# Pooling product of a hybrid decoder layer: fp32 operands, or operands split into two parts with three passes

## The chip, the cores and the metric

The kernel runs on one core of one Trainium2 chip. The metric is the device time of one execution in microseconds (us). A core has a matrix engine (PE, TensorE) with its weight loads (PEld), a vector engine (DVE), a scalar engine (ACT), a further engine (POOL) and one that mostly issues transfers (SP). The engines work side by side and wait for one another through semaphores.

## The reference

One decoder layer over 1024 positions of width 1024: a token-mixing sub-layer, a squared-ReLU MLP, and a last norm. The token mixing has a part that the change touches, a pooling mixer over 256 channels, and beside it a gated recurrence over 768 channels.

```python
def pool_mixer(u, w, scale):
    # u: (B, S, 256); w: (4, 64, 64); scale: (256,)
    for gi, win in enumerate((2, 4, 8, 16)):
        lo, hi = gi * 64, (gi + 1) * 64
        win_sum = c[:, :, lo:hi] - cp[:, MAX_WIN - win:MAX_WIN - win + S, lo:hi]
        cnt = jnp.minimum(t + 1, win)
        groups.append(win_sum / cnt - uf[:, :, lo:hi])
    p = jnp.stack(groups, axis=2)
    y = jnp.einsum('bsgc,gcd->bsgd', p, w).reshape(B, S, 256)
    return y * scale

h = rms_norm(x, norm_mix_g); u = h @ w_in
x = x + concat([pool_mixer(...), hgrn2_mixer(...)]) @ w_out
h2 = rms_norm(x, norm_mlp_g)
x = x + square(relu(h2 @ w_up)) @ w_down
return rms_norm(x, final_norm_g)
```

Here `c` is the running sum of the pooling inputs over positions: each output is the mean over a trailing window less the token itself, multiplied by a 64 x 64 matrix of its group. All inputs and the output are float32.

## The kernel before

The kernel works on tiles of 128 partitions. Its large products don't multiply fp32 operands directly. `split` (lines 116 to 119) makes two parts of an operand, a rounded high part with an ACT cast to fp32r and a low part with a DVE subtract, and `mm3` (lines 121 to 126) multiplies high by high, high by low and low by high into one PSUM bank: three matmuls, seen in the profile as lines 124, 125 and 126.

The work has three large stages. The first projects the normed input with `w_in` and runs the recurrence head by head (0 to 372 us of the span), with the output projection `w_out` at its end and after it. The second is the product with `w_up`, the third that with `w_down`.

In the first stage the six heads run one after another. Each head's recurrence (`hgrn`, line 394) is cut into the steps near, middle, far, keys, updates and output. Dense products that later heads need (`beside`, line 602) are dealt out between the steps by a table of lags, so TensorE has dense matmuls while DVE and ACT prepare the next step. The order on TensorE is written out by hand in all of this. The order on DVE and ACT is written out only in the opening part (lines 643 to 723), which ends with the first preparations of head 0; after it a planner places their instructions by its own estimate of when each is ready, and may also put prefetches between those of the opening part.

The pooling part has two tiles of 128 channels, `kt` 0 and 1. `pool_input` (line 555) loads its columns of `w_in` as a split weight, runs the dense product for both halves of the positions (shown as `ps_pool`), and builds the windows on DVE by doubling (lines 561 to 574), ending with a multiply-subtract at line 571. `pool_output` (line 577) multiplies the windows by `pw`, a block-diagonal 128 x 128 matrix that holds two groups, 512 positions at a time (line 581), and ACT scales the result into `mix` (line 584). Tile 0 is prepared beside head 4, and multiplied beside head 5, after the gate of head 4. Tile 1 is prepared next, and multiplied after 12 of the 16 steps of the gate of head 5. `pw` is zeroed at line 241 and loaded with four small transfers on SP at line 721.

The parts of weights live in a ring of four turns for each part (pool `wsplit`, line 152, tags `whi` and `wlo`, filled by `load_w`, line 156). From there the blocks of `w_out` come too: four blocks at lines 747 and 748, in the order that `MIX_ORDER` (line 37) needs them. The scores' PSUM banks (`score_ps`, two of them) are used by the pooling product as well.

After the last gate, `mix` is split into `mT` (line 752), and TensorE begins the output rows (`ps_o`), 2, 3 and 4 of the mixing blocks first, then the transposes of the last head, then blocks 5, 6, 0, 1 and 7.

Of the kernel before, what the change touches and what calls it, by code (L numbers as in the profile page):

```python
# [11 lines left out]
F32R = mybir.dt.float32r  # L12
# [5 lines left out]
P = 128  # L18
S = 1024
# [43 lines left out]
def kernel(  # L63
# [20 lines left out]
    pe, act, dve, pool = nc.tensor, nc.scalar, nc.vector, nc.gpsimd  # L84
# [31 lines left out]
    def split(hi, lo, src):  # L116

        act.copy(hi, src)  # L118
        dve.tensor_tensor(out=lo, in0=src, in1=hi.bitcast(F32), op=ALU.subtract)  # L119

    def mm3(ps, lhs, rhs, start, stop, goes_on=False):

        (lh, ll), (rh, rl) = lhs, rhs
        pe.matmul(ps, lh, rh, start=start, stop=False, skip_group_check=goes_on)  # L124
        pe.matmul(ps, lh, rl, start=False, stop=False, skip_group_check=goes_on)  # L125
        pe.matmul(ps, ll, rh, start=False, stop=stop, skip_group_check=goes_on)  # L126
# [24 lines left out]
    wring = {"raw": [], "split": [], "n": 0}  # L151
# [28 lines left out]
    with ExitStack() as pa:  # L180
        cmix = pa.enter_context(tc.tile_pool(name="cmix", bufs=1))
# [8 lines left out]
        lb = cmix.tile([P, NH], F32, name="lb")  # L190
        om = cmix.tile([P, NH], F32, name="om")
        pw = cmix.tile([P, 2, P], F32, name="pw")
        ha = pa.enter_context(tc.tile_pool(name="ha", bufs=2))
        HALF = S // 2
        V0 = POOL_W + 2 * HW
# [148 lines left out]
        def col_tile(c0, name, raw=None, parts=split):  # L344
            return load_w(w_in_v[:, :, c0:c0 + P], [KT, P], name, raw=raw, parts=parts)

        def dense_T(dst, w, h, name):

            ps = dense_ps(f"ps_{name}_{h}")
            for j in range(KT):  # L350
                mm3(ps, (w[0][:, j, :], w[1][:, j, :]), (hT[h][0][:, j, :], hT[h][1][:, j, :]), j == 0, j == KT - 1)
                yield
            rv, pv = rms_row[:, h * HALF:(h + 1) * HALF], ps
            if len(dst.shape) == 3:
                rv, pv = rv.rearrange("p (c t) -> p c t", t=P), pv.rearrange("p (c t) -> p c t", t=P)
            dve.tensor_tensor(out=dst, in0=pv, in1=rv, op=ALU.mult)
            return ps
# [197 lines left out]
        def pool_input(kt, wins):  # L555
            u = ha.tile([P, S], F32, tag="GQ"[kt], name=f"u_{kt}", bufs=1 + kt)
            w = col_tile(kt * P, f"pool{kt}")
            for h in range(2):
                yield from dense_T(by_chunk(u, h), w, h, f"pool{kt}")
            prev = u  # L560
            for lev in range(2 * kt + 2):
                sh = 1 << lev
                w = wins[lev % 2]
                dve.tensor_copy(w[:, :sh], prev[:, :sh])
                dve.tensor_tensor(out=w[:, sh:], in0=prev[:, sh:], in1=prev[:, :S - sh], op=ALU.add)
                prev = w
            for e in range(2):
                pr = slice(e * 64, (e + 1) * 64)
                w = wins[e]
                dve.tensor_tensor(out=w[pr, :PAD], in0=w[pr, :PAD], in1=pconst[pr, kt, :PAD], op=ALU.mult)  # L570
                dve.scalar_tensor_tensor(
                    out=wins[0][pr, :], in0=w[pr, :], scalar=pconst[pr, kt, PAD:], in1=u[pr, :],
                    op0=ALU.mult, op1=ALU.subtract,
                )
            return wins[0]

        def pool_output(kt, u):
            t = ha.tile([P, S], F32, tag="V", name=f"mix_{kt}", bufs=3)
            for b in range(2):
                ps = score_ps(f"psp_{kt}_{b}")  # L580
                pe.matmul(ps, pw[:, kt, :], u[:, b * 512:(b + 1) * 512], start=True, stop=True)
                for h in range(2):
                    c0 = h * 512 + b * 256
                    act.mul(
                        t[:, c0:c0 + 256].rearrange("p (c t) -> p c t", t=P), by_chunk(ps, h), pscale[:, kt:kt + 1]
                    )
            mix[kt] = t
# [55 lines left out]
        with tc.manual_schedule(engines={mybir.EngineType.PE, mybir.EngineType.DVE, mybir.EngineType.Activation}):  # L643
            for j in load_xt(0, (("Q", 2), ("Q", 2), ("K", 2), ("K", 2))):
                xt_hi(0, j)
                if j % 4 == 0:
                    raw = wraw.tile([P, 4, 256], F32, tag="raw", name=f"raw_v0_{j // 4}")
                    w0.append([wring["split"][0].tile([P, 4, 256], F32R, tag=f"w{part}", name=f"w{part}_v0_{j // 4}") for part in ("hi", "lo")])

                n = 1 if j < 2 else 2 if j % 2 == 0 else 0  # L650
                if n:
                    ks = slice(j % 4, j % 4 + n)
                    nc.sync.dma_start(raw[:, ks], w_in_v[:, j:j + n, V0:V0 + 256])
                    split(w0[-1][0][:, ks], w0[-1][1][:, ks], raw[:, ks])
                xt_lo(0, j)
            wq = q_weights(0, early_raw("T", "q_0"), put_off)
            xns = [load_rows(i) for i in range(2)]
            wf = f_weights(0, early_raw("Kn", "f0"), put_off)
            xns += [load_rows(i) for i in range(2, 4)]
            for _ in load_xt(1, (("F", 1), ("V", 3), ("G", 1), ("S", 1))):  # L660
                pass
            xns += [load_rows(i) for i in range(4, NT)]
            split(*later.pop(0))


            mx = small.tile([P, NH], F32, tag="lbt", name="lb_shift")
            dve.tensor_tensor(out=mx, in0=lbl, in1=lbl, op=ALU.subtract)
            ex = small.tile([P, NH], F32, tag="lbt", name="lb_exp")
            act.activation(ex, mx, AF.Exp)
            rc = small.tile([P, NH], F32, tag="lbt", name="lb_rcp")  # L670
            dve.reciprocal(rc, ex)
            sm = small.tile([P, NH], F32, tag="lbt", name="lb_soft")
            dve.tensor_tensor(out=sm, in0=ex, in1=rc, op=ALU.mult)
            dve.tensor_tensor(out=lb, in0=sm, in1=sm, op=ALU.subtract)
            dve.tensor_scalar(om, lb, -1.0, 1.0, op0=ALU.mult, op1=ALU.add)

            heads[0] = q, f, k = head_tiles(0)
            values(0)
            scales = row_scales(0, xns[:4])
            steps(scales, 2)  # L680
            split(*later.pop(0))
            steps(scales, 3)
            vps = finish(first_V(0, w0))
            work_q, work_f = gated(q, wq, 0, "q_0"), forget(f, k, wf, 0, 0)
            steps(work_q)
            steps(work_f)
            for j in range(KT):
                xt_hi(1, j)
                xt_lo(1, j)
                if j % 2 and j < 4:  # L690
                    scaled_V(0, vps[j // 2], j - 1)
                elif j == 5:
                    finish(scales)
            vps = finish(first_V(1, w0))
            finish(work_q)
            finish(work_f)

            pool.memset(ones, 1.0)
            mraw = ha.tile([P, len(LEVELS) * 2 + 1, 32], mybir.dt.int32, tag="Kn", name="mraw", bufs=1)
            nc.sync.dma_start(mraw, masks_in)  # L700
            for g in range(4):
                pr = slice(g * 32, (g + 1) * 32)
                act.copy(lmask[pr], mraw[pr, :2 * len(LEVELS) - 2, g % 2 * 16:g % 2 * 16 + 16])
            act.copy(dmask, mraw[:, 2 * len(LEVELS), :])
            scales = row_scales(1, xns[4:])
            steps(scales, 5)
            for e, ps in enumerate(vps):
                scaled_V(0, ps, 4 + 2 * e)
            ready_w["q"] = q_weights(1)
            work_q = gated(q, wq, 1, "q_0")  # L710
            steps(work_q)
            finish(scales)
            finish(work_q)
            ready_w["f"] = f_weights(1)
            finish(forget(f, k, wf, 1, 0))
            nc.sync.dma_start(pconst, pool_const)
            nc.sync.dma_start(pscale, pool_scale)
            nc.sync.dma_start(hg, hgrn_norm_g)
            for n in range(2):
                for e in range(2):  # L720
                    nc.sync.dma_start(pw[e * 64:(e + 1) * 64, n, e * 64:(e + 1) * 64], pool_w[0, 2 * n + e])
            chain = hgrn(0, *heads[0], vts[0])
            stage = next(chain)

# [396 lines left out]
    with ExitStack() as pd:  # L1121
# [105 lines left out]
        for at, (g, n) in enumerate(products[:-2]):  # L1227
            last = g == DOWN_GROUPS - 1
            pools, a, b = ahead
# [12 lines left out]
        with tc.manual_schedule(engines={mybir.EngineType.DVE, mybir.EngineType.Activation, mybir.EngineType.Pool}):  # L1242
            pools, a, b = ahead
# [74 lines left out]
```

## Time and profile before

| what | us |
|---|---|
| median of 3 runs | 1074.33 (1074.18 to 1074.35) |
| profiled execution | 1074.34 |
| its span | 1072.4 |
| TensorE busy | 1063.8 |
| DVE busy | 740.8 |
| ACT busy | 446.6 |
| POOL busy | 79.9 |

The span is what the profile shows, from the first to the last recorded instruction; the profiled execution's own time contains it. In rows of the timeline the first number is the start, the second the duration, both in us; then engine, line, operation, output and inputs, shape, count, and in brackets the idle time before it with what ended it. Instructions on one engine overlap a little, and matmuls overlap much: what counts for them is the distance from start to start. In rows of groups the count is followed by busy time and the mean in ns of one.

### The profile page before, as it was taken

What the parts mean: (1) busy time and instruction counts of PE and PEld (TensorE: products, weight loads), DVE (VectorE), ACT (ScalarE), POOL (GpSimd) and SP (SyncE); (2) the same over time, 40 slices, a digit from 0 to 9 for tenths busy, and PEclk for the clock granted to TensorE, in tenths of its full rate; (3) what the DMA queues carried; (4) which work ended last, traced back from release to release, by engine and by line L of the source; (5) the groups of instructions that cost most, each with busy time, mean ns of one, the idle gap of its engine ahead of it and who ended that gap; (6) DMA issues with size and microseconds to landing.
All of it is one profiled execution on the core that took longest, in us unless ns stands there. A gap on an engine that the chain in (4) does not pass through costs nothing.

```text
span 1072.4 us, 14951 instructions
## 1 busy us (share of the span) xinstructions
PE 1063.8 (99%) x6118; PEld 892.3 (83%) x6118; DVE 740.8 (69%) x922; ACT 446.6 (42%) x716; POOL 79.9 (7%) x125
## 2 busy tenths in 40 slices
PE   9999999999999999999999999999999999999997
PEld 7978898889888788888888888888888888888886
DVE  5488735764576823799856855876879878677775
ACT  7765444554434622473223223323425242423334
POOL 1010000100010111101001101100100000000001
PEclk9999999999999999999999999999999999999999
DMA  9421102110210444135434534428993244254104
GB/s 325 141 77 40 41 21 60 40 41 21 60 40 21 134 142 137 69 108 177 156 116 179 184 100 168 177 96 307 380 348 125 101 174 163 112 197 156 40 1 157
DMA packets 71540, 137.59 MB, mean 128 GB/s; under 512 B 5040, under 2 KB 45104, under 8 KB 67888
## 3 DMA queue, kind: packets, MB, share of 16 engines
q1 hardware_dynamic: 60688, 100.97, 27.8%
q0 software_dynamic: 9344, 33.56, 8.1%
q10 hardware_dynamic: 1440, 2.10, 0.5%
q8 instruction: 48, 0.79, 0.3%
q14 instruction: 20, 0.16, 0.1%
HBM read 98.87 MB, written 37.75 MB: 127 GB/s over the span
## 4 chain that ended last, share of the span: by engine, by line
PE 98%; DMA 0%; DVE 0%; ACT 0%; SPq 0%; issue 0%; POOL 0%; ACTq 0%
PE ps_ua L126 5%; PE ps_ua L125 5%; PE ps_ua L124 5%; PE ps_dx L124 5%; PE ps_dx L125 5%; PE ps_dx L126 5%; PE ps_o L126 3%; PE ps_o L124 3%; PE ps_o L125 3%; PE ps_uc L126 3%; PE ps_dy L124 3%; PE ps_uc L125 3%; PE ps_dy L125 3%; PE ps_dy L126 3%; PE ps_uc L124 3%; PE ps_f L124 2%
## 5 line engine op out<-in xcount | busy, mean ns | idle before, releaser
L118 ACT CAST wdop<-raw_wd 128x2048 fp32r<-128x2048 f32 x28 | 53.6, 1913 | 154.6 <-PE ps_dy L126 49.6
L124 PE MATMUL ps_ua<-h2op,whi_wu 128*128 128x512 f32 x256 | 99.8, 390 | 0.0
L126 PE MATMUL ps_ua<-h2op,wlo_wu 128*128 128x512 f32 x256 | 99.7, 389 | 0.0
L125 PE MATMUL ps_ua<-h2op,whi_wu 128*128 128x512 f32 x256 | 99.7, 389 | 0.0
L126 PE MATMUL ps_dx<-wdop,hop 128*128 128x512 f32 x252 | 98.1, 389 | 0.0
L124 PE MATMUL ps_dx<-wdop,hop 128*128 128x512 f32 x252 | 98.1, 389 | 0.0
L125 PE MATMUL ps_dx<-wdop,hop 128*128 128x512 f32 x252 | 98.1, 389 | 0.0
L119 DVE TENSOR_TENSOR wdop<-raw_wd,wdop 128x2048 fp32r<-128x2048 f32 x28 | 64.1, 2290 | 27.7 <-ACT wdop L118 27.7
L118 ACT CAST hop<-hraw 128x2048 fp32r<-128x2048 f32 x28 | 53.4, 1910 | 33.2 <-DMA hraw<-hid 21.4
L119 DVE TENSOR_TENSOR hop<-hraw,hop 128x2048 fp32r<-128x2048 f32 x28 | 64.0, 2284 | 3.0 <-ACT hop L118 3.0
L118 ACT CAST whi_wu<-wsum 128x1024 fp32r<-128x1024 f32 x22 | 23.2, 1054 | 93.2 <-PE ps_ub L126 27.5
L119 DVE TENSOR_TENSOR wlo_wu<-raw_wu,whi_wu 128x1024 fp32r<-128x1024 f32 x23 | 28.0, 1222 | 47.5 <-ACT whi_wu L118 47.5
L801 DVE TENSOR_TENSOR x<-ps_dx,x 128x512 f32<-128x512 f32 x64 | 43.9, 688 | 18.7 <-PE ps_dx L126 18.7
L125 PEld LDWEIGHTS ps_ua<-h2op,whi_wu 128*128 128x128 f32 x256 | 48.1, 188 | 10.0
L124 PEld LDWEIGHTS ps_ua<-h2op,whi_wu 128*128 128x128 f32 x256 | 48.1, 188 | 10.0
L126 PEld LDWEIGHTS ps_ua<-h2op,wlo_wu 128*128 128x128 f32 x256 | 48.1, 188 | 9.9
L126 PEld LDWEIGHTS ps_dx<-wdop,hop 128*128 128x128 f32 x252 | 47.3, 188 | 9.9
L124 PEld LDWEIGHTS ps_dx<-wdop,hop 128*128 128x128 f32 x252 | 47.3, 188 | 9.8
L125 PEld LDWEIGHTS ps_dx<-wdop,hop 128*128 128x128 f32 x252 | 47.3, 188 | 9.7
L1034 POOL DMA_DIRECT2D hid<-hid x56 | 29.8, 532 | 283.5 <-DVE hid L1031 216.5
L126 PE MATMUL ps_uc<-h2op,wlo_wu 128*128 128x512 f32 x128 | 49.8, 389 | 0.0
L125 PE MATMUL ps_dy<-wdop,hop 128*128 128x512 f32 x128 | 49.8, 389 | 0.0
(271 smaller groups left out, 2771.2 us busy)
## 6 DMA issues: line engine op xcount, KB each, us to landing
hid<-hid POOLq DMA_DIRECT2D x56, 512.0 KB, 3.3
hraw<-hid SPq DMA_DIRECT2D x28, 1024.0 KB, 5.3
raw_wu<-in_w_up_dram SPq DMA_DIRECT2D x32, 512.0 KB, 3.7
raw_wd<-in_w_down_dram SPq DMA_DIRECT2D x16, 1024.0 KB, 7.2
xt<-in_x_t_dram SPq DMA_DIRECT2D x16, 256.0 KB, 5.9
xn<-in_x_dram SPq DMA_DIRECT2D x8, 512.0 KB, 7.5
x<-x_mid SPq DMA_DIRECT2D x8, 512.0 KB, 5.6
raw_q<-in_w_in_dram SPq DMA_DIRECT2D x6, 512.0 KB, 4.0
```

Of the source, the lines that this page charges most:

```text
L118: act.copy(hi, src)
L119: dve.tensor_tensor(out=lo, in0=src, in1=hi.bitcast(F32), op=ALU.subtract)
L124: pe.matmul(ps, lh, rh, start=start, stop=False, skip_group_check=goes_on)
L125: pe.matmul(ps, lh, rl, start=False, stop=False, skip_group_check=goes_on)
L126: pe.matmul(ps, ll, rh, start=False, stop=stop, skip_group_check=goes_on)
L801: dve.tensor_tensor(out=out_, in0=a, in1=b, op=ALU.add)
L1034: nc.gpsimd.dma_start(store[n][:, at, :], t)
```

## The change

`pw` gets two parts of its own, `pw_hi` and `pw_lo`, split once in the opening part, right behind the transfers that load it and ahead of the first work of head 0. `pool_input` no longer hands on the windows in fp32: it takes a turn of the weight ring for each of the two parts, and splits the windows into them in two halves of 512 positions. `pool_output` multiplies the parts with `mm3`.

```diff
         pw = cmix.tile([P, 2, P], F32, name="pw")
+        pws = [cmix.tile([P, 2, P], F32R, name=f"pw_{part}") for part in ("hi", "lo")]
...
-            return wins[0]
+            parts = [wring["split"][0].tile([P, S], F32R, tag=f"w{part}", name=f"w{part}_win_{kt}") for part in ("hi", "lo")]
+            for h in range(2):
+                cs = slice(h * HALF, (h + 1) * HALF)
+                split(parts[0][:, cs], parts[1][:, cs], wins[0][:, cs])
+            return parts
...
                 ps = score_ps(f"psp_{kt}_{b}")
-                pe.matmul(ps, pw[:, kt, :], u[:, b * 512:(b + 1) * 512], start=True, stop=True)
+                mm3(ps, [w[:, kt, :] for w in pws], [part[:, b * 512:(b + 1) * 512] for part in u], True, True)
...
                     nc.sync.dma_start(pw[e * 64:(e + 1) * 64, n, e * 64:(e + 1) * 64], pool_w[0, 2 * n + e])
+            split(*pws, pw)
             chain = hgrn(0, *heads[0], vts[0])
```

## The prediction

> **What bounds the kernel now.** I read the page first (busy time, then the chain that ended last), then the waits of TensorE alone.
>
> ```profile
> PE 1063.8 (99%) x6118; PEld 892.3 (83%) x6118; DVE 740.8 (69%) x922; ACT 446.6 (42%) x716; POOL 79.9 (7%) x125
> ...
> PE 98%; DMA 0%; DVE 0%; ACT 0%; SPq 0%; issue 0%; POOL 0%; ACTq 0%
> ```
>
> ```profile
> PE warm L225 <- DVE junk L223: 1.2, 1, 1.2
> PE ps_v L277 <- DVE wlo_v L119: 0.3, 1, 0.3
> ```
>
> TensorE is the chain from its first matmul to its last, and it waits for other engines 1.5 us in all. Two things follow. Time that TensorE itself saves is saved in full. And since its order is fixed by hand, time that it is made to wait is lost in full: hardly any later wait is there to shrink. So the question is what TensorE saves at the two pooling products, and whether the new vector and scalar work makes it wait anywhere.
>
> All sums stand against the profiled execution: span 1072.4 us, run 1074.34 us, 1.94 us around the span. The median of the three runs is 1074.33, so nothing has to be shifted.
>
> **The saving.** The timeline around the first pooling product (start, duration, engine, line):
>
> ```profile
> 325.10 0.40 PE L126 MATMUL ps_g<-hT_hi,wlo_g 128*128 128x512 f32 x1
> 325.34 1.88 PE L581 MATMUL psp<-win,pw 128*128 128x512 f32 x4
> 326.65 0.80 PE L124 MATMUL ps_pool<-hT_hi,whi_pool 128*128 128x512 f32 x1
> 327.29 0.40 PE L125 MATMUL ps_pool<-hT_lo,whi_pool 128*128 128x512 f32 x1
> 327.52 0.40 PE L126 MATMUL ps_pool<-hT_hi,wlo_pool 128*128 128x512 f32 x1
> ```
>
> Two fp32 matmuls of 512 columns show as four records, so each takes two passes. A matmul of a split product starts 0.23 us after the one before (327.29 to 327.52 here). Without the pooling product the ps_pool L125 would have started two such steps after 325.10, at 325.56; it started at 327.29. The product therefore costs 1.73 us, the turn from fp32 back to split passes included. The changed product has 2 x 3 = 6 passes: 6 x 0.23 = 1.38 us. Saved: 0.35 us per product. The second product has the same four records, and I take the same for it: the two save **0.7 us**.
>
> The trace has no split pass on these very operands. From below, a pass can't be shorter than its weight load; from above, it is no longer than a pass of the fp32 form.
>
> ```profile
> L581 PEld LDWEIGHTS psp<-winK,pw x4: 188/188/189, 355.1 to 356.2; 128*128 128x128 f32 x4
> ```
>
> At 0.188 us the twelve passes take 2.26 us instead of 3.46: 1.2 us saved. At the fp32 pass's step (1.73 / 4 = 0.43) they take 5.2: 1.7 us lost. I take 0.23, since the form is that of every dense product here.
>
> The Trainium skill (FP8 and Floating Point Precision, TensorE Precision Notes) says true fp32 takes four passes through the array. By four passes at the dense step, sixteen would become twelve and 0.92 us would be saved. The trace shows two longer records per matmul, and their measured 1.73 us stays in the sum.
>
> **The split of the pooling weights.** It is one ACT cast and one DVE subtract of 128x256, in the stretch whose ACT and DVE order is written out. It stands behind the last forget work of head 0 and ahead of the first work of `hgrn(0)`. Its input has long landed: SP issued the four loads of `pw` from 34.65 us, and the slowest took 3.3 us.
>
> ```profile
> 34.65 3.36 SPq L721 DMA_DIRECT2D pw<-in_pool_w_dram  x4
> ```
>
> ```profile
> 54.97 0.73 ACT L370 ACTIVATE K<-K,om 128x512 f32<-128x512 f32 x1
> ...
> 61.26 0.66 ACT L411 COPY kq<-Q 128x512 f32<-128x512 f32 x1
> 61.92 0.70 ACT L412 COPY kq<-K 128x512 f32<-128x512 f32 x1
> ```
>
> ```profile
> 55.73 1.23 DVE L399 TENSOR_TENSOR d<-Q,K 128x1024 f32<-128x1024 f32 x1 [0.74 <-ACT K L370]
> ...
> 58.21 1.22 DVE L119 TENSOR_TENSOR wlo_q<-raw_q,whi_q 128x1024 fp32r<-128x1024 f32 x1
> 59.34 0.69 DVE L402 TENSOR_TENSOR d<-Q,K 128x512 f32<-128x512 f32 x1
> 59.94 0.68 DVE L356 TENSOR_TENSOR Q<-ps_q,rms_row 128x512 f32<-128x512 f32 x1
> ...
> 61.14 0.69 DVE L532 TENSOR_TENSOR K<-K,F 128x512 f32<-128x512 f32 x1
> ```
>
> ```profile
> 61.89 0.86 PE L392 MATMUL sc_near<-d,ones 128*32 128x256 f32 x16
> 62.67 0.46 PE L420 MATMUL sc_near<-kq 128*32 128x32 f32 x32
> ```
>
> DVE starts `d` (L399) as soon as ACT has made `k` (55.70), and from there to the second key copy (L412, ends 62.62) nothing is idle: DVE is back to back, and ACT copies as soon as Q and K are there. TensorE's L420 matmul starts at 62.67, 0.05 us behind that copy, and the view of the tile `kq` lists a wait of its weight load:
>
> ```profile
> PEld sc_near L420: 0.2, 1
> ```
>
> So there is no slack. The two operations have rows of the same size and types elsewhere:
>
> ```profile
> L118 ACT CAST whi_v<-raw_v 128x256 fp32r<-128x256 f32 x2 | 0.8, 397 | 0.0
> ...
> L119 DVE TENSOR_TENSOR wlo_v<-raw_v,whi_v 128x256 fp32r<-128x256 f32 x2 | 0.9, 426 | 4.2 <-ACT whi_v L118 4.2
> ```
>
> The cast can't start before L370 ends, in ACT's order. The subtract waits for the cast, and L399 stands behind the subtract. So L399 moves by about 0.40 + 0.43, less some 0.1 by which neighbours overlap on these engines (59.34 to 59.94 is 0.60 for a duration of 0.69): 0.7 us. All of the DVE chain behind it moves too, and TensorE waits **0.7 us** at L420. Bounds: nothing, if the planner takes the weight subtract at 58.21 (1.13 us, needed only by the next head) out of the chain; 1.3 us, if another 0.60 us filler goes in ahead of L532. I take 0.7, as every link is in written order. What follows is late by as much as TensorE is, so it finds its old slack.
>
> **The splits of the windows.** Each product adds two ACT casts and two DVE subtracts of 128x512: 0.61 and 0.69 us (0.60 when back to back).
>
> ```profile
> L118 ACT CAST mT_hi<-mix 128x512 fp32r<-128x512 f32 x16 | 9.0, 614 | 9.3 <-PE ps_g L125 5.8 <-DVE mix L545 3.5
> ...
> L119 DVE TENSOR_TENSOR mT_lo<-mix,mT_hi 128x512 fp32r<-128x512 f32 x16 | 10.2, 690 | 0.0
> ```
>
> ```profile
> 318.07 2.59 DVE L571 SCALAR_TENSOR_TENSOR win<-win,pconst,u 64x1024 f32<-64x1024 f32 x2
> ...
> 351.03 1.28 DVE L571 SCALAR_TENSOR_TENSOR winK<-winF,pconst,u 64x1024 f32<-64x1024 f32 x1
> ```
>
> The first windows are done at 320.66, and TensorE takes them at 325.34: 4.7 us for a cast and two subtracts, about 2. The second are done at 352.31 and taken at 355.34: 3.0 us for the first half's 1.3. Even if DVE did 1.7 us of other work in between, the low part would come about when the second pass asks for it. I cost both at **0**; uncovered, each would cost up to 1.3 us, a cast and a subtract in a row. The cover is the gate product that TensorE runs meanwhile.
>
> **The weight ring.** The parts take turns in the four-deep ring of weight parts. Each block waits for the one four turns back, so two more turns move the blocks behind. The casts of the w_out blocks show the old turns (the second of the four came at 325, when the gate product above ended):
>
> ```profile
> 313.12 1.05 ACT L118 CAST whi_wo<-raw_wo 128x1024 fp32r<-128x1024 f32 x1 [1.72 <-PE ps_pool L125]
> ...
> 342.33 1.05 ACT L118 CAST whi_wo<-raw_wo 128x1024 fp32r<-128x1024 f32 x1
> ...
> 359.80 1.06 ACT L118 CAST whi_wo<-raw_wo 128x1024 fp32r<-128x1024 f32 x1 [1.19 <-PE ps_g L125]
> ```
>
> Counted four back in the new order, the first three become about 325 (behind the weights of that gate), 342 (behind the second pooling weights) and 357 (behind the second product's parts, which TensorE is through with by then); the fourth stays at the last gate's end. So one more block's cast and subtract (1.05 and 1.13 us) falls between 352 and 364, beside the second window split's 1.2 us on DVE: 2.3 us more, of which two waits for POOL take up 1.8.
>
> ```profile
> 356.60 0.69 DVE L521 TENSOR_TENSOR on<-po,rstd_o 128x512 f32<-128x512 f32 x1 [0.90 <-POOL rstd_o L133]
> ...
> 358.86 0.69 DVE L521 TENSOR_TENSOR on<-po,rstd_o 128x512 f32<-128x512 f32 x1 [0.90 <-POOL rstd_o L133]
> ...
> 363.07 1.22 DVE L119 TENSOR_TENSOR wlo_wo<-raw_wo,whi_wo 128x1024 fp32r<-128x1024 f32 x1
> ...
> 364.80 4.30 DVE L119 TENSOR_TENSOR mT_lo<-mix,mT_hi 128x512 fp32r<-128x512 f32 x7
> ```
>
> ```profile
> 367.94 0.23 PE ps_o L125
> ```
>
> The last block's low part ends at 364.29, and TensorE asks for it at 367.94 (block of j = 0). Half a microsecond later it is still 3 us early: **0**. No load is added; the fourth block's load waits on SP for the second block's subtract, as it did for the third's before.
>
> Sum: 1074.34 - 0.70 + 0.70 + 0 + 0 = **1074.3 us**.
>
> **Rivals.**
> - *The saving stands.* DVE's order closes the 0.7 us gap at L399, and TensorE doesn't wait at 62.7: 1074.34 - 0.70 = 1073.6. For it: the filler at 58.21 isn't in written order. Against it: it was placed there before. 0.20.
> - *A product waits for its split.* The planner puts other work ahead of it, at 352 above all, where DVE is back to back: 0.6 to 1.3 us, so 1074.9 to 1075.6. 0.09.
> - *The ring makes it slower.* The fourth w_out subtract slips behind the seven mT subtracts (4.2 us, rows above) and ends near 364.3 + 0.5 + 4.2 = 369.0, or 370.4 if the two `mix` operations (1.4 us) go first as well. It decides from 367.94 on; the loss is 1.1 to 2.5 us, so up to 1076.8. Against it: the planner set that subtract ahead of them before. 0.07.
> - *The change doesn't do what it says*: passes on these operands run at the fp32 step. +1.7 and +0.7 give 1076.7. Every split row speaks against it. 0.02.
>
> The forecast has 0.55; 0.07 is left for reordered work elsewhere that TensorE feels (0.02 faster, 0.02 unseen, 0.03 slower).
>
> **How the numbers follow.** 1074.3 is the likeliest case. The range goes from 1073.1 (passes at the weight load's pace, no wait: 1074.34 - 1.2) to 1076.2 (the forecast with the wait of 1.3 instead of 0.7 and one product uncovered: 1074.3 + 0.6 + 1.3). It takes in the forecast, the saving alone, the uncovered product and most of the ring. What this kernel's measurement can tell from no change is about 0.2%, 2.1 us: 1072.2 to 1076.5. No named case reaches 1072.2: faster 0.02, from reordering. Slower: the upper part of the ring (0.03), the fp32 step (0.02) and reordering (0.03) make 0.08. The same: 0.90.
>
> **What would show it.** Right: six L124 to L126 records per pooling product within 1.4 us, and about 0.7 us of idle or stretched TensorE ahead of L420 near 62.7, with L399 starting near 56.4. Wrong: L399 still near 55.7, or L420 without delay (then 1073.6); a wait of TensorE on the window parts near 325 or 355; ps_o near 368 waiting for `wlo_wo`. A change of more than 2 us either way would come from a place that I didn't see.

## The result, and the profile after

| | before | changed kernel |
|---|---|---|
| median of the runs, us | 1074.26 | 1098.89 |
| its runs, us | 1073.84 to 1074.35 | 1098.18 to 1099.59 |
| ratio, 95% interval | | 1.023 (1.0212 to 1.0248) |
| span of the profiled execution, us | 1072.4 | 1097.4 |

The change is slower by 24.6 us, where no difference was forecast. The page of the changed kernel, busy times and the chain that ended last, and then TensorE's waits for other engines:

```profile
PE 1068.5 (97%) x6122; PEld 896.6 (82%) x6122; DVE 744.3 (68%) x927; ACT 448.7 (41%) x721; POOL 79.3 (7%) x125
...
PE 91%; ACT 3%; DVE 2%; DMA 2%; issue 1%; SPq 0%; POOL 0%; ACTq 0%; POOLq 0%
```

```profile
PE ps_g L124 <- ACT whi_g L118: 19.1, 2, 10.6
PE sc_near L421 <- ACT kq L413: 1.4, 1, 1.4
PE warm L226 <- DVE junk L224: 1.2, 1, 1.2
```

TensorE now stands still for 19.1 us in two waits, and both are for the same thing: the high part of a gate's weights (`whi_g`). Neither product itself nor its windows are in this list. Line numbers of the changed kernel are a little higher than before (L420 is now L421, L531 L532 and so on).

Where TensorE stands in the timeline of the changed kernel:

```profile
314.23 0.39 PE L126 MATMUL ps_pool<-hT_hi,wlo_pool 128*128 128x512 f32 x1
323.13 0.80 PE L124 MATMUL ps_g<-hT_hi,whi_g 128*128 128x512 f32 x1 [8.52 <-ACT whi_g L118]
323.73 0.63 PE L125 MATMUL ps_g<-hT_lo,whi_g 128*128 128x512 f32 x1
...
327.12 0.63 PE L126 MATMUL ps_g<-hT_hi,wlo_g 128*128 128x512 f32 x1
327.55 0.56 PE L124 MATMUL ps_g<-hT_hi,whi_g 128*128 128x512 f32 x1
327.95 0.39 PE L125 MATMUL ps_g<-hT_lo,whi_g 128*128 128x512 f32 x1
...
366.74 0.80 PE L124 MATMUL ps_g<-hT_hi,whi_g 128*128 128x512 f32 x1 [10.59 <-ACT whi_g L118]
```

And ACT, which makes these weights, in the same stretch:

```profile
271.36 1.05 ACT L118 CAST whi_pool<-raw_pool 128x1024 fp32r<-128x1024 f32 x1 [1.48 <-PE ps_v L126]
321.00 1.14 ACT L118 CAST whi_win<-win 128x512 fp32r<-128x512 f32 x2 [8.78 <-DVE win L572]
322.04 1.04 ACT L118 CAST whi_g<-raw_g 128x1024 fp32r<-128x1024 f32 x1
322.99 1.04 ACT L118 CAST whi_pool<-raw_pool 128x1024 fp32r<-128x1024 f32 x1
364.60 1.14 ACT L118 CAST whi_win<-winK 128x512 fp32r<-128x512 f32 x2 [10.04 <-DVE winK L572]
365.64 1.04 ACT L118 CAST whi_g<-raw_g 128x1024 fp32r<-128x1024 f32 x1
366.59 1.04 ACT L118 CAST whi_wo<-raw_wo 128x1024 fp32r<-128x1024 f32 x1
```

There is a pattern. Each gate's weights come right behind a split of windows, and ACT was idle for 8.78 and 10.04 us ahead of those. In the kernel before, the same casts came at these times:

```profile
272.50 1.06 ACT L118 CAST whi_g<-raw_g 128x1024 fp32r<-128x1024 f32 x1
284.26 1.05 ACT L118 CAST whi_pool<-raw_pool 128x1024 fp32r<-128x1024 f32 x1 [0.69 <-PE ps_q L125]
298.83 1.05 ACT L118 CAST whi_g<-raw_g 128x1024 fp32r<-128x1024 f32 x1 [3.97 <-PE ps_f L125]
```

The first of these gates is that of head 4, the second that of head 5. The first gate's cast went from 272.5 to 322.0 although its data was there: SP issued its load at 247.27 in the changed kernel, and the loads of these weights took 3.8 to 4.2 us to land.

```profile
247.27 0.37 SPq L161 DMA_DIRECT2D raw_g<-in_w_in_dram  x1
```

The waits cost more than their own length. Here are the windows view's rows for the two stretches behind them (TensorE's busy time, other engines, and third from the right the granted clock):

```profile
323.20:328.00 4.80, 4.76 (x11) 3.31 (x12) 2.27 (x2) 0.83 (x1) 0.00 (x0) 0.51 0.48 137
...
366.80:372.00 5.20, 5.16 (x11) 3.59 (x12) 2.28 (x2) 0.83 (x1) 0.00 (x0) 0.50 0.55 182
```

After each wait the granted clock is about half for some 5 us. Behind the first, ten passes took 4.82 us (323.13 to 327.95) instead of 10 x 0.23 = 2.3: 2.5 us more, the first few of them waiting for the low part as well. The Trainium skill (TensorE: Matmul & The Clock Gate, Part 1) says that the clock falls to half after an idle window of about 3.4 us and comes back after a busy one. The trace agrees: idle for 8.5 and 10.6 us, then 0.51 and 0.50. But a wait of 1.6 us, shorter than that window, cost the clock too in one of the runs below (e6, last section); there the measurement decides.

Following single instructions from one trace to the other gives the account. The first matmul after `kq` of head 0 is 1.3 us late (63.06 to 64.39). The last `ps_pool` of tile 0 is still 1.3 late (312.92 to 314.23). The transposes behind the first product are 12.2 late (329.15 to 341.39): 11.3 for the first wait (8.5, 2.5, and the empty pipeline), less the product's saving. The product of tile 1 starts 25.9 late (355.34 to 381.25): 13.6 for the second wait (10.6, and 2.9 for twelve slow passes). Its saving and 0.6 us picked up in the remaining 700 us leave the span's 25.0.

### The profile page after: what moved, and what is told of

Same layout as the page of the kernel before. It is cut to its first block, busy times and chain, and to the rows that moved or that the text cites. A ratio compares the mean times of both kernels' runs of the same rounds, so it can differ in the third digit from the quotient of the medians.

```text
span 1097.4 us, 14968 instructions
## 1 busy us (share of the span) xinstructions
PE 1068.5 (97%) x6122; PEld 896.6 (82%) x6122; DVE 744.3 (68%) x927; ACT 448.7 (41%) x721; POOL 79.3 (7%) x125
## 4 chain that ended last, share of the span: by engine, by line
PE 91%; ACT 3%; DVE 2%; DMA 2%; issue 1%; SPq 0%; POOL 0%; ACTq 0%; POOLq 0%
PE ps_ua L124 5%; PE ps_ua L126 5%; PE ps_ua L125 5%; PE ps_dx L126 5%; PE ps_dx L125 5%; PE ps_dx L124 5%; PE ps_o L125 3%; PE ps_o L126 3%; PE ps_o L124 3%; PE ps_uc L124 3%; PE ps_dy L126 3%; PE ps_dy L125 3%; PE ps_uc L126 3%; PE ps_uc L125 3%; PE ps_dy L124 3%; PE ps_g L124 2%
## 5 line engine op out<-in xcount | busy, mean ns | idle before, releaser
L124 PE MATMUL ps_g<-hT_hi,whi_g 128*128 128x512 f32 x96 | 40.8, 425 | 19.1 <-ACT whi_g L118 19.1
L532 DVE TENSOR_TENSOR Q<-Q,dec 128x512 f32<-128x512 f32 x36 | 25.0, 695 | 38.4 <-ACT kq L412 34.5
```

The costliest lines, as they stand in the source:

```text
L532: dve.tensor_tensor(out=queries(q, m), in0=queries(q, m), in1=sibling(t_m, False, m), op=ALU.mult)
```

## The experiments

Three theories could explain waits on the gate's weights. *Order*: a turn of the ring is given out only when its first write can be placed, and later turns don't pass it; so the gate's weights, which the program asks for after the windows' parts, wait for windows that are done at 321 us. *Depth*: two more turns are simply too many for four slots. *Load*: the casts and subtracts that came in keep ACT and DVE from making the weights.

### e1_early_write: the parts' turns taken early

```diff
             parts = [wring["split"][0].tile([P, S], F32R, tag=f"w{part}", ...) for part in ("hi", "lo")]
+            act.copy(parts[0][:, :4], nhalf[:, :4])
+            dve.tensor_copy(parts[1][:, :4], nhalf[:, :4])
```

> The change with one addition: each of the window's parts gets a write of four columns right after its turn in the ring is taken, from data that is there from the start (overwritten later by the split). Order theory (a turn of the ring is given out only when its first write can be placed, and later turns can't pass it, so the gate's weights stood behind a write that can't come before the windows are done at 321 us): the early write takes the turn near 272 us, the weights of both gates and of the second pooling tile come in time, no wait of TensorE on whi_g, 1074.3 to 1076. Depth theory (four slots are too few for two more turns): the same turns in the same order, held even longer, so TensorE waits for whi_g as in the change, 1095 to 1101. Load theory (the added casts and subtracts themselves delay the gate weights on ACT and DVE): no change, 1097 to 1100.

Measured: 1077.78 us, ratio 1.0031 (1.002 to 1.0042). The waits on `whi_g` are gone. ACT's casts in this run:

```profile
272.85 0.21 ACT L577 CAST whi_win<-nhalf 128x4 fp32r<-128x4 f32 x1
284.60 1.05 ACT L118 CAST whi_g<-raw_g 128x1024 fp32r<-128x1024 f32 x1 [0.68 <-PE ps_q L125]
299.17 1.05 ACT L118 CAST whi_pool<-raw_pool 128x1024 fp32r<-128x1024 f32 x1 [3.97 <-PE ps_f L125]
313.46 0.19 ACT L577 CAST whi_win<-nhalf 128x4 fp32r<-128x4 f32 x1 [1.72 <-PE ps_pool L125]
320.03 1.15 ACT L118 CAST whi_win<-win 128x512 fp32r<-128x512 f32 x2 [1.21 <-DVE win L572]
325.77 1.03 ACT L118 CAST whi_g<-raw_g 128x1024 fp32r<-128x1024 f32 x1
```

Writes of four columns are all that was added (on ACT at 272.85 for tile 0 and at 313.46 for tile 1), and the first gate's cast comes at 284.60, as soon as the query weights four turns back are released. The second comes at 325.77, behind the parts of tile 0. There are as many turns in the same order, held longer, and as much work: depth and load fall. The time is 1.8 us above the expected top. The profile has a new wait, and behind it the granted clock was 0.50 from 374 to 376 us:

```profile
PE ps_o L124 <- ACT mT_hi L118: 2.7, 1, 2.7
```

### e2_parts_later: the turns behind the gate's

```diff
-            parts = [wring["split"][0].tile([P, S], F32R, ...) for part in ("hi", "lo")]
+            return wins[0]
+
+        def pool_output(kt, win):
+            u = [wring["split"][0].tile([P, S], F32R, ...) for part in ("hi", "lo")]
             for h in range(2):
                 cs = slice(h * HALF, (h + 1) * HALF)
-                split(parts[0][:, cs], parts[1][:, cs], wins[0][:, cs])
-            return parts
-
-        def pool_output(kt, u):
+                split(u[0][:, cs], u[1][:, cs], win[:, cs])
```

> The change with the window's parts taken from the ring, and split, at the head of pool_output, so that their turns come behind those of the gate's weights. Order theory: the waits on whi_g are gone; the w_out blocks now stand behind the second tile's parts and crowd behind 352 us, so 1074.5 to 1079, with any wait of TensorE near 360 to 370. Depth theory: as many turns through four slots, so at least half of the loss stays, 1086 to 1100. Load theory: as much work at the same time, 1095 to 1100.

Measured: 1079.24 us, ratio 1.0047 (1.0032 to 1.0062), 0.2 us above the range of the order theory and far below the others. No wait on `whi_g`. The second tile's and the second gate's weights are still held, now behind the split of tile 0's windows: their casts came at 284.26 and 298.83 before. TensorE needs them late enough not to wait:

```profile
320.16 1.14 ACT L118 CAST whi_win<-win 128x512 fp32r<-128x512 f32 x2 [1.20 <-DVE win L572]
321.80 1.04 ACT L118 CAST whi_pool<-raw_pool 128x1024 fp32r<-128x1024 f32 x1
324.83 1.05 ACT L118 CAST whi_g<-raw_g 128x1024 fp32r<-128x1024 f32 x1
```

The w_out blocks are behind a late write too, the split of tile 1's windows at 352.97 us:

```profile
355.29 1.06 ACT L118 CAST whi_wo<-raw_wo 128x1024 fp32r<-128x1024 f32 x1
358.41 1.12 ACT L118 CAST whi_wo<-raw_wo 128x1024 fp32r<-128x1024 f32 x1
```

```profile
PE ps_o L124 <- ACT mT_hi L118: 2.8, 1, 2.8
...
PE ps_o L125 <- DVE wlo_wo L119: 0.7, 1, 0.7
```

The wait of 0.7 us ends at 368.7, where that theory put it; the one of 2.8 us ends at 374.3, a little behind.

### e3_own_places: no turn at all

```diff
-            parts = [wring["split"][0].tile([P, S], F32R, tag=f"w{part}", ...) for part in ("hi", "lo")]
+            tags = (("K", 2), ("Q", 2)) if kt == 0 else (("pair", 3), ("pair", 3))
+            parts = [ha.tile([P, S], F32R, tag=tag, ..., bufs=n) for part, (tag, n) in zip(("hi", "lo"), tags)]
```

> The change with the window's parts in places that are free at that time (tags K and Q for tile 0, pair for tile 1) and not in the ring; products, splits and the weights' split as in the change. Order theory and depth theory: no wait on whi_g, only the 1.4 us at sc_near of head 0 against 0.7 us saved, 1074.3 to 1075.5. Load theory: 1095 to 1100.

Measured: 1075.87 us, ratio 1.0017 (1.0008 to 1.0026). All of the new work is there, and 23 of the 24.6 us are gone. Load falls again. It is 0.4 us above the expected top. Its waits are not the expected ones: none is listed at `sc_near`, where 1.4 us was expected, and `ps_o` waits 1.6 us for `mT_hi`.

### e4_turns_alone: the turns, and the old product

```diff
-        pws = [cmix.tile([P, 2, P], F32R, name=f"pw_{part}") for part in ("hi", "lo")]
...
-            return parts
+            return wins[0]
...
-                mm3(ps, [w[:, kt, :] for w in pws], [part[:, b * 512:(b + 1) * 512] for part in u], True, True)
+                pe.matmul(ps, pw[:, kt, :], u[:, b * 512:(b + 1) * 512], start=True, stop=True)
...
-            split(*pws, pw)
```

`pool_input` hands on the fp32 windows again; the parts are written and not read.

> The kernel before with the change's two turns and the splits of the windows into them, but nothing reads the parts: the product stays fp32, and pw isn't split. Order theory: both waits on whi_g are there as in the change, since they come from when the parts are written and not from how long they are held; 1096 to 1099. Depth theory: the parts give up their slots as soon as they are written, so the second gate's weights and the w_out blocks find slots earlier; a loss well below the change's, 1080 to 1094. Theory that the three passes are slow: no loss, 1074 to 1076.

Measured: 1098.95 us, ratio 1.0232 (1.0214 to 1.0249): the changed kernel's time. The waits are the same, to the tenth:

```profile
PE ps_g L124 <- ACT whi_g L118: 19.1, 2, 10.6
```

So the loss needs neither the three passes nor the split of `pw`, and not that the parts are held. Together with e1, which moves only the first write, it comes from when they are first written.

### e5 and e6: the split of the pooling weights

The small terms follow. e5 is the kernel before plus `split(*pws, pw)`:

> The kernel before with nothing added but the split of pw into its parts where the change has it (nothing reads them). Chain theory (the written chain from k to the key copy of head 0 has no slack, so a cast and a subtract in it make TensorE wait at sc_near): a wait of TensorE on the key copy near 62.7 us, 1074.6 to 1075.8 against 1074.4 before. Rival (the wait that the change shows there came from loads that arrived later in that execution, not from the split): no wait beyond the kernel before's, 1074.2 to 1074.6.

e6 is e3 with that split traced in `pool_input` instead, so that it is no longer in the written order:

```diff
         def pool_input(kt, wins):
+            if kt == 0:
+                split(*pws, pw)
...
-            split(*pws, pw)
             chain = hgrn(0, *heads[0], vts[0])
```

> As e3_own_places, with the split of pw out of the written order: it is traced in pool_input, and the planner has it on ACT behind the squares of the second half and on DVE ahead of the second query weights, where both wait near 43 us. Chain theory: no wait at sc_near near 62.7, and 0.2 to 1.4 us less than e3_own_places. Together with the saving of 0.7 us and the wait of 1.6 us of ps_o on the last mT cast that e3_own_places shows: 1074.4 - 0.7 + 1.6 = 1075.3. Rival (the wait at sc_near isn't the split's): as e3_own_places, 1075.9.

Measured: e5 1075.11 us against 1074.47, ratio 1.0004 (0.9994 to 1.0013); e6 1075.56, ratio 1.001 (1.0001 to 1.0019). By its rows the split does what was worked out. In the changed kernel `k` ends at 56.51, and DVE's `d` starts 0.67 us later, where it was 0.03 before:

```profile
55.78 0.73 ACT L371 ACTIVATE K<-K,om 128x512 f32<-128x512 f32 x1
56.41 0.39 ACT L118 CAST pw_hi<-pw 128x256 fp32r<-128x256 f32 x1
```

```profile
56.83 0.43 DVE L119 TENSOR_TENSOR pw_lo<-pw,pw_hi 128x256 fp32r<-128x256 f32 x1 [1.02 <-ACT pw_hi L118]
57.18 1.22 DVE L400 TENSOR_TENSOR d<-Q,K 128x1024 f32<-128x1024 f32 x1
```

The stretch from the end of `k` to the end of the key copy that TensorE waits for takes 7.44 to 7.47 us in the five kernels that have the split in this place (the changed one, e1, e2, e3, e5), and 6.87 to 6.93 us in the six that don't (before, e4, e6 to e9). So the split makes this chain 0.5 us longer. What TensorE then waits at `sc_near` goes also with when `k` ends, and that is 55.1 to 56.8 us in these profiles, with the split or without. With the split the wait was 1.4 us in the changed kernel, 0.4 in e1 and e5, 0.2 in e2 and not listed in e3; without it 1.1 in e7, where `k` ends last, 0.3 in e9, 0.2 in e6, where the split is at 42.5 us and out of the way, and not listed in the others. In the changed kernel the loads of the opening were about 0.8 us later than before (SP's first `raw_g` at 49.32 instead of 48.50) and `k` with them, so 0.8 of the 1.3 us that TensorE is late there isn't the split's. The times agree in sign, with 0.6 us for e5 and 0.3 from e3 to e6 (whose 1075.56 lies between its two forecasts, 1075.3 and 1075.9), and neither is clear of the noise.

### e7, e8 and e9: the wait of ps_o

e7 is e6 with DVE's order written out at the stage's end:

```diff
-        with tc.manual_schedule(engines={mybir.EngineType.PE}):
+        with tc.manual_schedule(engines={mybir.EngineType.PE, mybir.EngineType.DVE}):
             first_rows = {i: bank(f"ps_o_0_{i}") for i in range(2)}
...
             products_out(first_rows, left_weight, MIX_ORDER[3:])
-        for j in MIX_ORDER:
-            mix_split(1, j)
+            for j in MIX_ORDER:
+                mix_split(1, j)
```

> As e6_weights_split_in_gap, with DVE's order at the stage's end written out: the splits of mT's second half stand behind the two mix operations of the last head and their split, instead of ahead of them. DVE theory (the second tile's subtracts push the last head's mix operations later on a DVE that is back to back there, and ps_o waits for their cast): the wait of ps_o on mT_hi is gone, 1074.4 - 0.7 = 1073.7. ACT theory (the added casts on ACT are what makes the last cast late): the wait stays, 1075.3.

e8 is e6 with the fp32 product and unsplit windows for tile 1 (`if kt: return wins[0]`, and the old matmul):

> As e6_weights_split_in_gap, but the second tile keeps its fp32 product and its windows aren't split. DVE theory: no wait of ps_o on mT_hi beyond the kernel before's, half of the saving, 1074.4 - 0.35 = 1074.0. Rival (the wait of ps_o comes from the first tile's work or from the moved orders, not from the second tile's subtracts): the wait stays, 1075 to 1076.

e9 has the order of e7 on the kernel before:

> The kernel before (fp32 pooling product, no splits of it) with the stage's end in the written DVE order of e7_last_head_first. It tells whether e7's gain over the kernel before comes from that order or from the split product. Theory that the gain is the split product's 0.7 us: no wait stood there before, so no difference, 1074.2 to 1074.7. Theory that the order gains by itself: 1073.0 to 1073.9.

| kernel | median, us | before, us | ratio (95%) | wait of ps_o on mT_hi, us |
|---|---|---|---|---|
| e6 | 1075.56 | 1074.47 | 1.001 (1.0001 to 1.0019) | 1.6 |
| e7 | 1073.0 | 1074.47 | 0.9986 (0.9977 to 0.9995) | none |
| e8 | 1073.9 | 1074.47 | 0.9996 (0.9987 to 1.0005) | none |
| e9 | 1073.85 | 1074.25 | 0.9996 (0.9987 to 1.0005) | none |

DVE at the end of the stage, in e6:

```profile
364.28 5.50 DVE L119 TENSOR_TENSOR mT_lo<-mix,mT_hi 128x512 fp32r<-128x512 f32 x9
369.70 1.40 DVE L546 SCALAR_TENSOR_TENSOR mix<-pto,hg,g 128x512 f32<-128x512 f32 x2
```

and in e7:

```profile
366.71 1.40 DVE L546 SCALAR_TENSOR_TENSOR mix<-pto,hg,g 128x512 f32<-128x512 f32 x2
368.15 5.51 DVE L119 TENSOR_TENSOR mT_lo<-mix,mT_hi 128x512 fp32r<-128x512 f32 x9
```

In e6 nine subtracts stand in a row ahead of the last head's `mix`. In e7 seven of them (the splits of `mT`'s second half) stand behind it, with the last head's own two, and the wait is gone. Without tile 1's subtracts (e8) there is none either. So it is DVE's queue, not ACT's casts. e7 is faster than the kernel before by 1.5 us, with an interval of 0.5 to 2.5, and 0.7 us below its forecast. How much of it is the product's and how much the order's is open. e9 shows 0.4 us for the order alone, which lies in the range of the theory that the order gains by itself, but within the noise; e8 shows 0.6 for half of the product with the old order, within the noise as well.

## Why the prediction was wrong

**The saving was right.** In the changed kernel's timeline the six passes take the place from 337.91 to 339.31 and from 381.25 to 382.65, 1.40 us each instead of 1.73: 0.66 us together, for 0.7 forecast. The passes run at the dense step; neither the weight load's pace nor the fp32 step shows.

```profile
337.91 0.40 PE L124 MATMUL psp<-whi_win,pw_hi 128*128 128x512 f32 x1
...
339.31 0.40 PE L124 MATMUL ps_pool<-hT_hi,whi_pool 128*128 128x512 f32 x1
```

**The split of the pooling weights was right in its mechanism.** `d` moves by 0.64 us for 0.7 forecast, and the key copy ends 0.5 us later behind `k`. The prediction took `k` to end at the same time in every execution; it varies by more than the split costs. TensorE's wait there was 1.4 us in the profiled execution, mostly from later loads, so the size of what the split costs in time isn't pinned down.

**The splits of the windows hid what they were said to hide, and hit another place.** TensorE waits for no part at either product, also in e1 and e3, where the products come near their old times. But 1.2 us more on DVE ahead of the last head's `mix` makes `ps_o` wait 1.6 us once the large loss is out of the way (e3, e6). The prediction checked the last w_out block near 368 and missed the block behind it: the row at 364.80 showed seven subtracts on DVE, the two `mix` operations come right behind them at 369.01, ACT casts each as soon as it is there, and TensorE's first matmul on them starts at 370.48, about when the first cast ends. There was no slack at all. In the kernel before:

```profile
369.01 1.41 DVE L545 SCALAR_TENSOR_TENSOR mix<-pto,hg,g 128x512 f32<-128x512 f32 x2
```

```profile
369.80 1.28 ACT L118 CAST mT_hi<-mix 128x512 fp32r<-128x512 f32 x2 [3.46 <-DVE mix L545]
```

```profile
370.48 0.50 PE L124 MATMUL ps_o<-whi_wo,mT_hi 128*128 128x512 f32 x1
```

**The weight ring is the step that failed.** Its term was 0, and the runs show 19.1 us of waits there. The prediction said that each block waits for the one four turns back, and counted when slots come free; so it looked only at the w_out blocks, at the end. It took a turn to be no more than a slot, held from when it is free. The runs show a second condition: the turn is given out with its first write, in traced order. The gate's and the second tile's weights come behind the parts in that order, so they were held for a write that can't be placed before 321 us, and again before 365. With the early write of e1 the w_out casts came at 328.7, 342.4, 358.1 and 360.1; the prediction had counted about 325, 342 and 357 and the last gate's end. So its count of slots was right, once the first write doesn't come late. The rival of a slower ring was likewise put at the wrong end, at the fourth w_out subtract, with a price of 2.5 us at most.

**The range** took its upper end from a doubled opening wait and an uncovered product. A wait of TensorE long enough to lose its clock wasn't among the cases. The two waits with the slow passes behind them are 24.9 us here: 11.3 and 13.6.

That the planner holds later turns back is inferred from the order in which ACT got its work; ACT stood idle for 8.78 us with the gate's data loaded. Whether a fifth slot would have helped wasn't tried.

## What to carry to other kernels

Before a tile joins a ring, ask not only which slots it takes but when it is first written, and what comes behind it in traced order: a late first write holds up every later turn, prefetches for the busiest engine among them. If it has to share the ring, take its turn behind the prefetches, or write a few columns early; places of its own were better here (1079.2, 1077.8 and 1075.9 us). And when an engine with a full queue gets more work, look at every later thing that TensorE takes from that queue, the last one first.

## What was not expected of the hardware

The granted clock fell in both waits (its mean was 0.70 from 314.0 to 323.2 us and 0.62 from 356.0 to 366.8), and TensorE ran slowly for 4.8 us and 5.6 us of matmuls behind them, mostly at 0.43 us per pass instead of 0.23. With the wait of the first passes for the low part this is 2.5 and 2.9 us on top of the waits.

A short wait can cost the clock or not. Around the wait of 1.6 us in e3 the windows view gives a granted clock of 1.00 (third number from the right), so it cost only itself.

```profile
364.00:374.00 10.00, 8.41 (x39) 6.40 (x38) 9.09 (x15) 4.78 (x8) 0.00 (x0) 1.00 0.74 233
```

In e6 a wait of the same length at the same place, which ended at 371.1, was followed by half clock:

```profile
373.00:376.00 3.00, 3.00 (x9) 2.33 (x8) 2.31 (x3) 1.37 (x3) 0.76 (x1) 0.50 0.91 268
```

Eight passes from 372.9 to 376.3 us took 0.43 us each instead of 0.23: 1.6 us more, as much as the wait itself. This execution was the longest of e6's (1076.52 us, the median is 1075.56). What decides between the two cases no run here shows.
